# A streaming row normalisation on one core: one queue with a fixed order of whole 8 MB loads and stores

## The chip, the cores and the metric

One core of one Trainium2 chip. The metric is the device time of one execution in microseconds (us). The kernel before took 318.35 us (median of 3 runs, 318.33 to 318.56). The profile that is read here is one execution taken by the hardware profiler; its span (316.9 us for the kernel before) is about 1.5 us shorter than the timed figure.

Names used throughout: L0 to L7 are the eight loads of a tile (8 MB each, HBM to on-chip memory), S0 to S7 the eight stores of the same tiles. A "change of direction" is a place in the queue where a load follows a store or a store follows a load. In the profile lines DVE is VectorE, ACT is ScalarE and SPq the queue of the sync engine; "x4" counts instructions; q1 is the queue that carries the data and q14 the one that fetches instructions, each with packets, MB and share of the time of the 16 DMA engines. The trace does not number the 16 engines: a packet is put to the engine whose packet before ended where this one starts.

## The reference

```
x: float32 [32, 512, 1024]
sums = sum(abs(x), axis=-1, keepdims=True)
out  = x / (sums + 1e-8)
```

Each of 16,384 rows of 1,024 numbers is divided by its sum of absolute values. 67.1 MB are read and 67.1 MB written; there is little arithmetic.

## The kernel before

A tile is 128 partitions x 16 rows x 1,024 numbers: 64 KB in each partition, 8 MB in all. There are three buffers, so at most three tiles are on the chip. The scheduler of the framework decides in which order the queue of the sync engine gets the transfers.

```python
BUFS = 3
# ...
def process_chunk(x_tile, out_ap, r0, rN, mv):
    s = stats.tile([P, rN], mybir.dt.float32, tag="s")
    nc.vector.tensor_reduce(out=s[:, :], in_=x_tile[:, r0 : r0 + rN, :],
        axis=mybir.AxisListType.X, op=mybir.AluOpType.add, apply_absolute_value=True)
    inv = stats.tile([P, rN], mybir.dt.float32, tag="inv")
    nc.vector.reciprocal(out=inv[:, :], in_=s[:, :])
    for r in range(rN):
        # rows r < mv on VectorE (tensor_scalar_mul), the others on ScalarE (activation Copy, scale)
        # ...
    nc.sync.dma_start(out=out_ap[:, r0 : r0 + rN, :], in_=x_tile[:, r0 : r0 + rN, :])

MV = 10
for i in range(ntiles):
    x_tile = sbuf.tile([P, R, d], x.dtype)
    nc.sync.dma_start(out=x_tile[:, :, :], in_=x_t[i, :, :, :])
    if i < ntiles - 2:
        process_chunk(x_tile, out_t[i], 0, R, MV)
    else:                                   # last two tiles: four quarters, each stored by itself
        C = 4
        for c0 in range(0, R, C):
            process_chunk(x_tile, out_t[i], c0, C, (MV * C) // R)
```

The order that came out of it in the queue is L0 L1 L2 S0 S1 S2 L3 L4 L5 S3 S4 S5 L6 L7, then S6 and S7 in quarters: 5 changes of direction.

## Time and profile before

| what | kernel before |
|---|---|
| timed, median | 318.35 us |
| span of the profile | 316.9 us |
| DMA engines busy (16 engines) | 98.6% |
| VectorE busy | 190.8 us, 60% |
| ScalarE busy | 56.7 us, 18% |

The page of the kernel before: the DMA rows over 40 equal slices of the span (tenths busy, then GB/s), the queues, and the chain that ended last.

```profile
DMA  9999999999999999999999999999999999999797
GB/s 397 397 397 513 414 397 397 397 438 488 397 397 505 422 397 397 521 405 397 480 447 397 397 489 438 397 430 480 414 397 480 438 405 422 399 431 432 335 430 331
...
q1 hardware_dynamic: 3168, 134.22, 98.6%
q14 instruction: 2, 0.02, 0.0%
...
DVE 57%; DMA 35%; issue 4%; ACT 0%; ACTq 0%; SPq 0%; DVEq 0%
```

The transfers are the limit: the DMA row is full from the first slice nearly to the last. That the chain names VectorE for 57% does not contradict this; it follows semaphores, and while VectorE worked on one tile the queue was still moving others. A packet is booked in the slice where it starts, so single slices swing around the mean of 424 GB/s.

The same kernel in stretches around its tail. Columns: from:to, length, busy time of VectorE, ScalarE and GpSimd with instructions, granted clock, DMA share, GB/s.

```profile
292.00:294.00 2.00, 2.00 (x4) 0.00 (x0) 0.00 (x0) 1.00 0.86 369
294.00:296.00 2.00, 2.00 (x4) 1.85 (x2) 0.00 (x0) 1.00 0.67 287
296.00:298.00 2.00, 2.00 (x1) 2.00 (x3) 0.00 (x0) 1.00 0.94 393
...
300.00:302.00 2.00, 1.97 (x5) 0.75 (x1) 0.00 (x0) 1.00 0.81 344
```

Near 294 and 300 us the DMA engines run dry for a moment: VectorE is busy throughout and the next quarter store is not ready. This is the only visible idle time after the start.

The groups of instructions by shape: busy us and mean ns of one, then idle time before and its releaser.

```profile
L37 DVE TENSOR_REDUCE s<-x_tile 128x16 f32<-128x16384 f32 x6 | 103.3, 17214 | 67.4 <-DMA x_tile<-in_x_dram 67.4
L54 ACT ACTIVATE x_tile<-x_tile,inv 128x1024 f32<-128x1024 f32 x52 | 55.4, 1137 | 223.9 <-DVE inv L45 223.9
L48 DVE TENSOR_SCALAR x_tile<-x_tile,inv 128x1024 f32<-128x1024 f32 x76 | 51.4, 748 | 0.3
L37 DVE TENSOR_REDUCE s<-x_tile 128x4 f32<-128x4096 f32 x8 | 35.0, 4399 | 43.8 <-DMA x_tile<-in_x_dram 43.8
```

A reduction of a quarter costs 4.40 us, a row 0.75 us on VectorE (0.67 when they follow each other) and 1.14 us on ScalarE. Small changes of the arithmetic can be costed from these.

### The profile page before, as it was taken

Reading aid. Unit: us, or ns where it says so; the run is one execution under the profiler, and the core shown is the slowest. Engines: PE = TensorE matmul, PEld = TensorE weight load, DVE = VectorE, ACT = ScalarE, POOL = GpSimd, SP = SyncE. Lnnn points to the kernel's source line nnn. Section 1 sums busy time; section 2 is a strip of 40 time slices with the busy share of each in tenths; the row PEclk is TensorE's granted clock in tenths of the full one; section 3 lists DMA queues with packets and bytes.
Section 4 is the critical chain, followed back from the end, with each engine's and each line's share of the span. In section 5 each row is a group of like instructions: output and inputs, shape, how many; then the busy total and the mean of one; then the engine's idle time right before and its main releaser. Section 6 shows DMA issues by size and latency. Waiting matters only on the chain.

```text
span 316.9 us, 261 instructions
## 1 busy us (share of the span) xinstructions
DVE 190.8 (60%) x104; ACT 56.7 (18%) x53; POOL 0.2 (0%) x4
## 2 busy tenths in 40 slices
DVE  0019999999990000039999999980000069999910
ACT  0010080080080000000160070080000002522520
POOL 0000000000000000000000000000000000000000
DMA  9999999999999999999999999999999999999797
GB/s 397 397 397 513 414 397 397 397 438 488 397 397 505 422 397 397 521 405 397 480 447 397 397 489 438 397 430 480 414 397 480 438 405 422 399 431 432 335 430 331
DMA packets 3170, 134.24 MB, mean 424 GB/s; under 512 B 352, under 2 KB 352, under 8 KB 352
## 3 DMA queue, kind: packets, MB, share of 16 engines
q1 hardware_dynamic: 3168, 134.22, 98.6%
q14 instruction: 2, 0.02, 0.0%
HBM read 67.11 MB, written 67.11 MB: 424 GB/s over the span
## 4 chain that ended last, share of the span: by engine, by line
DVE 57%; DMA 35%; issue 4%; ACT 0%; ACTq 0%; SPq 0%; DVEq 0%
DVE s L37 41%; DMA x_tile<-in_x_dram 35%; DVE x_tile L48 15%; DVE inv L45 1%; ACT x_tile L54 0%; ACTq L99 0%; SPq L60 0%; DVEq L45 0%; DVEq L48 0%
## 5 line engine op out<-in xcount | busy, mean ns | idle before, releaser
L37 DVE TENSOR_REDUCE s<-x_tile 128x4 f32<-128x4096 f32 (+1 forms) x14 | 138.3, 9891 | 111.2 <-DMA x_tile<-in_x_dram 111.2
L54 ACT ACTIVATE x_tile<-x_tile,inv 128x1024 f32<-128x1024 f32 x52 | 55.4, 1137 | 223.9 <-DVE inv L45 223.9
L48 DVE TENSOR_SCALAR x_tile<-x_tile,inv 128x1024 f32<-128x1024 f32 x76 | 51.4, 748 | 0.3
L54 ACT ACT_TABLE_LOAD x1 | 1.3, 1283 | 22.8 <-DMA x_tile<-in_x_dram 22.8
L45 DVE RECIPROCAL inv<-s 128x4 f32<-128x4 f32 (+1 forms) x14 | 2.6, 200 | 0.4
L88 POOL MEMSET const-bfloat16-1.0<- 128x1 bf16 x1 | 0.1, 101 | 0.0
L88 POOL MEMSET const-uint8-127<- 128x1 uint8 x1 | 0.1, 101 | 0.0
L88 POOL MEMSET const-float32-0.0<- 128x1 f32 x1 | 0.1, 98 | 0.2 <-issue 0.2
L88 POOL MEMSET const-float32-1.0<- 128x1 f32 x1 | 0.1, 98 | 0.0
## 6 DMA issues: line engine op xcount, KB each, us to landing
out_dram<-x_tile SPq DMA_DIRECT2D x8, 2048.0 KB, 9.9
x_tile<-in_x_dram SPq DMA_DIRECT2D x8, 51.0
out_dram<-x_tile SPq DMA_DIRECT2D x6, 29.5
```

What stands on the lines that cost most here:

```text
L37: nc.vector.tensor_reduce(out=s[:, :], in_=x_tile[:, r0 : r0 + rN, :], axis=mybir.AxisListType.X, op=mybir.AluOpType.add, apply_absolute_v ...
L45: nc.vector.reciprocal(out=inv[:, :], in_=s[:, :])
L48: nc.vector.tensor_scalar_mul(out=x_tile[:, r0 + r, :], in0=x_tile[:, r0 + r, :], scalar1=inv[:, r : r + 1],)
L54: nc.scalar.activation(out=x_tile[:, r0 + r, :], in_=x_tile[:, r0 + r, :], func=mybir.ActivationFunctionType.Copy, scale=inv[:, r : r + 1],)
L88: nc = _bacc.Bacc("TRN2", target_bir_lowering=False, num_devices=1)
```

## The change

Its intent: fix the order of the transfers by hand, so that each is a whole 8 MB transfer and so that each store and each load is ready when its turn comes. The last two loads go ahead of the third-last store (the exchange at the end of the plan). All tiles are computed in four chunks, with three rows of four on VectorE, and the epsilon of the reference is added.

```diff
-    stats = ctx.enter_context(tc.tile_pool(name="stats", bufs=BUFS))
+    stats = ctx.enter_context(tc.tile_pool(name="stats", bufs=4))
@@ compute, for every tile
+    C = 4
+    DVE_ROWS = 3
+        for c0 in range(0, R, C):
             # ... tensor_reduce of 4 rows
+            nc.vector.tensor_scalar_add(out=s[:, :], in0=s[:, :], scalar1=EPS)
             # ... reciprocal; 3 rows on VectorE, 1 on ScalarE
@@ order
+    plan = [("L", i) for i in range(BUFS)]
+    for i in range(ntiles):
+        plan.append(("S", i))
+        nxt = i + BUFS - 1
+        if BUFS <= nxt < ntiles:
+            plan.append(("L", nxt))
+    last = max(k for k, p in enumerate(plan) if p[0] == "L")
+    before = plan[last - 1]
+    plan[last - 1], plan[last] = plan[last], before
+    with tc.manual_schedule():
+        for what, i in plan:
+            if what == "L":
+                load(i)
+                compute(i)
+            else:
+                store(i)
```

The resulting order is L0 L1 L2 S0 S1 L3 S2 L4 S3 L5 S4 L6 L7 S5 S6 S7: 9 changes of direction.

More of the change, by code (lines that the diff above doesn't have):

```diff
@@ L7 @@
 from concourse._compat import with_exitstack
+FP32 = mybir.dt.float32
+EPS = 1e-8
 @with_exitstack
@@ L26 @@
     ntiles = n // (P * R)
+    BUFS = 3
     x_t = x_flat.rearrange("(n p r) d -> n p r d", p=P, r=R)
     out_t = out_flat.rearrange("(n p r) d -> n p r d", p=P, r=R)
-    BUFS = 3
     sbuf = ctx.enter_context(tc.tile_pool(name="sbuf", bufs=BUFS))
-    stats = ctx.enter_context(tc.tile_pool(name="stats", bufs=BUFS))
-    def process_chunk(x_tile, out_ap, r0, rN, mv):
-        s = stats.tile([P, rN], mybir.dt.float32, tag="s")
-        nc.vector.tensor_reduce(
-            out=s[:, :],
-            in_=x_tile[:, r0 : r0 + rN, :],
-            axis=mybir.AxisListType.X,
-            op=mybir.AluOpType.add,
-            apply_absolute_value=True,
-        )
-        inv = stats.tile([P, rN], mybir.dt.float32, tag="inv")
-        nc.vector.reciprocal(out=inv[:, :], in_=s[:, :])
-        for r in range(rN):
-            if r < mv:
-                nc.vector.tensor_scalar_mul(
-                    out=x_tile[:, r0 + r, :],
-                    in0=x_tile[:, r0 + r, :],
-                    scalar1=inv[:, r : r + 1],
-                )
-            else:
-                nc.scalar.activation(
-                    out=x_tile[:, r0 + r, :],
-                    in_=x_tile[:, r0 + r, :],
-                    func=mybir.ActivationFunctionType.Copy,
-                    scale=inv[:, r : r + 1],
-                )
-        nc.sync.dma_start(out=out_ap[:, r0 : r0 + rN, :], in_=x_tile[:, r0 : r0 + rN, :])
@@ L62, with load @@
-    MV = 10
-    for i in range(ntiles):
-        x_tile = sbuf.tile([P, R, d], x.dtype)
-        nc.sync.dma_start(out=x_tile[:, :, :], in_=x_t[i, :, :, :])
-        if i < ntiles - 2:
-            process_chunk(x_tile, out_t[i], 0, R, MV)
-        else:
-            C = 4
-            for c0 in range(0, R, C):
-                process_chunk(x_tile, out_t[i], c0, C, (MV * C) // R)
+    stats = ctx.enter_context(tc.tile_pool(name="stats", bufs=4))
+    tiles = {}
+    def load(i):
+        x_tile = sbuf.tile([P, R, d], FP32)
+        nc.sync.dma_start(out=x_tile[:, :, :], in_=x_t[i])
+        tiles[i] = x_tile
@@ new lines, in store, with compute @@
+    def store(i):
+        nc.sync.dma_start(out=out_t[i], in_=tiles[i][:, :, :])
+    C = 4
+    DVE_ROWS = 3
+    def compute(i):
+        x_tile = tiles[i]
+        for c0 in range(0, R, C):
+            s = stats.tile([P, C], FP32)
+            nc.vector.tensor_reduce(
+                out=s[:, :],
+                in_=x_tile[:, c0 : c0 + C, :],
+                axis=mybir.AxisListType.X,
+                op=mybir.AluOpType.add,
+                apply_absolute_value=True,
+            )
+            nc.vector.tensor_scalar_add(out=s[:, :], in0=s[:, :], scalar1=EPS)
+            inv = stats.tile([P, C], FP32)
+            nc.vector.reciprocal(out=inv[:, :], in_=s[:, :])
+            for r in range(C):
+                row = x_tile[:, c0 + r, :]
+                if r < DVE_ROWS:
+                    nc.vector.tensor_scalar_mul(out=row, in0=row, scalar1=inv[:, r : r + 1])
+                else:
+                    nc.scalar.activation(
+                        out=row,
+                        in_=row,
+                        func=mybir.ActivationFunctionType.Copy,
+                        scale=inv[:, r : r + 1],
+                    )
```

## The prediction

> **What bounds it now.** The DMA engines. The page's DMA row reads 9 in nearly all of 40 slices, and the queue table gives 98.6% of 16 engines' span (316.9 us) for 134.22 MB. Reading the packet records of the trace one by one: a 64 KB packet takes 2.418 us, a 16 KB packet 0.611 us. That is 27.1 GB/s per engine, 434 GB/s for 16, beside the 435 GB/s that the Trainium skill, "DMA: Bandwidth & Descriptors", section Specifications, calls the fabric ceiling: the trace agrees.
>
> So the floor is 128 packets of 64 KB per engine: 128 x 2.418 = 309.5 us. The other 7.4 us of the span, from the packet records:
> - start, until the first packets flow: about 2.0
> - first 16 packets slow (about 3.1 us each): 0.7
> - first change from loads to stores, at 58 us: 16 packets of about 3.65 us: 1.2
> - slow packets at later changes of direction: 0.5
> - idle at 293 and at 300 us, where quarter stores were not yet ready: 1.2 in the mean
> - 16 KB packets instead of 64 KB (4 x 0.611 against 2.418): 0.4
> - end, from last packet to end of span: 1.3
>
> The chain of waits says 57% VectorE, but the queue always held more work. VectorE is busy 190.8 us (60%).
>
> **What the change does.**
> 1. The queue becomes L0 L1 L2 S0 S1 L3 S2 L4 S3 L5 S4 L6 L7 S5 S6 S7, whole 8 MB transfers of 19.35 us. Saves 0.4, and, if nothing stalls, the 1.2 idle.
> 2. Direction changes go from 5 to 9. Later ones cost about 0.1 each: adds 0.4.
> 3. VectorE: reduces in four pieces, 4 x 4.39; 12 rows instead of 10 (0.672 each in sequence); four reciprocals at 0.17 and four epsilon adds, estimated at 0.17 too, plus gaps of 0.03. About 27.1 us per tile against 24.2; total about 217 us. ACT drops to 32 x 1.137 = 36 us. All hidden while a tile's load plus store take 38.7.
>
> **Is there a stall?** By queue position, with starts above: L2 ends near 61, S0 is ready at 50, S1 at 77, before its turn at 81. L3 waits for S0's landing at 81, with S1 behind it in the queue until 100. Later transfers are ready in time until the last. L6, twelfth, lands at about 237; tiles 6 and 7 need 54.2 us of VectorE, so S7 is issued at about 291.3 and flows 1 to 1.8 us later (as the first load did). S6 ends at about 294.3. Margin: 1 to 2 us. Without the swap, L7 would land 19.35 us later and S7 come about 7 us late.
>
> **Predicted:** 2.0 + 309.5 + 2.7 + 1.3, about 315.6 us of span, plus 1.45 (318.35 timed against 316.9 profiled): 317.0 us, 0.4% less. 8 in 10: 315.9 to 318.9. Faster by over 2% 0.01 (312 lies below floor plus start and end), within 2% 0.97, slower 0.02.
>
> **What would show it.** DMA share near 99%; packets of 64 KB only at 2.418 us; no gaps after the first packet, the last store following S6 without one; VectorE near 217 us; about 24 us after the last VectorE row rather than 13.
>
> **What would make it wrong.** A tile's compute above about 27.8 us: each us more shows twice in the tail, less the margin. Direction changes costing 1.2 us like the one at 58: up to 9 us more.

## The result

The changed kernel took 319.82 us (median of 5, 319.55 to 320.08) beside 318.40 us for the kernel before (318.33 to 318.67). The ratio is 1.0042 (95% interval 1.0030 to 1.0055). Ratios here and below are the mean time of one kernel's fast runs over that of the other's of the same rounds, so not quite the ratio of the medians. Run again later on another occasion, the changed kernel gave 1.0028 (1.0016 to 1.0040). So the change makes it 0.3 to 0.4% slower, where 0.4% faster (317.0 us) was predicted.

The page of the changed kernel, the same lines:

```profile
DMA  9999999999999999999999999999999999999996
GB/s 387 404 396 511 412 396 420 371 478 437 404 413 486 420 396 437 470 404 404 429 470 404 429 462 429 396 437 470 412 420 453 445 388 445 478 396 396 412 404 264
...
q1 hardware_dynamic: 2304, 134.22, 98.4%
q14 instruction: 2, 0.02, 0.0%
...
DVE 51%; DMA 29%; another core or an unknown queue 11%; issue 1%; DVEq 0%; SPq 0%
```

The DMA row looks as full as before, and 864 packets fewer (3,168 to 2,304: no quarter stores) bring no gain.

The tail of the changed kernel, before its last store and at its end:

```profile
292.00:294.00 2.00, 1.83 (x4) 0.59 (x1) 0.00 (x0) 1.00 0.76 328
294.00:296.00 2.00, 1.48 (x3) 0.56 (x1) 0.00 (x0) 1.00 0.23 98
296.00:298.00 2.00, 0.00 (x0) 0.00 (x0) 0.00 (x0) 1.00 1.23 524
...
313.00:314.00 1.00, 0.00 (x0) 0.00 (x0) 0.00 (x0) 1.00 2.27 983
314.00:315.00 1.00, 0.00 (x0) 0.00 (x0) 0.00 (x0) 1.00 0.15 66
```

Two things are to be seen. First, there is an idle gap before S7 after all (DMA share 0.23 from 294 to 296 us). Second, look at the last two lines: 983 GB/s for 1 us is fifteen 64 KB packets that start in the same microsecond, and 66 GB/s for 1 us is exactly one more packet, about 1 us later. One of the 16 DMA engines runs behind the others, and it ends the kernel.

Its groups of instructions:

```profile
L54 DVE TENSOR_REDUCE s<-x_tile 128x4 f32<-128x4096 f32 x32 | 141.2, 4413 | 73.6 <-DMA x_tile<-in_x_dram 73.6
L67 DVE TENSOR_SCALAR x_tile<-x_tile,inv 128x1024 f32<-128x1024 f32 x96 | 66.5, 749 | 1.1
L69 ACT ACTIVATE x_tile<-x_tile,inv 128x1024 f32<-128x1024 f32 x32 | 36.8, 1150 | 233.5 <-DVE inv L63 233.5
L63 DVE RECIPROCAL inv<-s 128x4 f32<-128x4 f32 x32 | 5.7, 178 | 3.0
L61 DVE TENSOR_SCALAR s<-s 128x4 f32<-128x4 f32 x32 | 5.4, 170 | 1.1
```

The arithmetic is as costed: VectorE 216.6 us in all against 217 predicted, an epsilon addition 0.17 us. And two lines of its timeline (start us, us, engine):

```profile
229.13 66.75 SPq L45 DMA_DIRECT2D out_dram<-x_tile  x3
...
239.98 4.42 DVE L54 TENSOR_REDUCE s<-x_tile 128x4 f32<-128x4096 f32 x1 [10.91 <-DMA x_tile<-in_x_dram]
```

VectorE could begin tile 6 at 239.98 us, where 237 had been expected, and S7, the last of the three stores in the first line, was issued at 295.5 (229.13 + 66.75 less its own 0.33) instead of 291.3.

The trace records when each of the 16 DMA engines has landed its share of a transfer. The distance between the first and the last of the 16 is the spread of the engines:

| spread of the 16 landings, us, by position in the queue | 1st | 4th | 8th | 12th | 14th | last |
|---|---|---|---|---|---|---|
| kernel before | 0.75 | 0.75 | 0.75 | 0.67 | 1.61 | 0.18 (a quarter) |
| changed kernel | 0.86 | 1.08 | 2.66 | 3.75 | 3.42 | 1.12 |

In the kernel before the spread stays under 1.1 us until the last loads, and falls from 1.67 to 0.25 us at 300 us, where all engines wait for a quarter store and start afresh. In the changed kernel it grows to 3.75 us. A load counts as landed only when the slowest engine is done. The Trainium skill, "DMA: Bandwidth & Descriptors", section "Why a DMA increments its semaphore by 16 and not by 1", says this: only the full count of 16 means that all data landed. The trace agrees: the twelfth transfer (L6) landed on its first engine at 236.21 us and on its last at 239.95, and VectorE began at 239.98.

### The profile page after: what moved, and what is told of

Same layout as the page of the kernel before. It is cut to its first block, busy times and chain, and to the rows that moved or that the text cites. A ratio compares the mean times of both kernels' runs of the same rounds, so it can differ in the third digit from the quotient of the medians.

```text
span 318.0 us, 336 instructions
## 1 busy us (share of the span) xinstructions
DVE 216.6 (68%) x192; ACT 38.1 (12%) x33; POOL 0.2 (0%) x4
## 3 DMA queue, kind: packets, MB, share of 16 engines
q1 hardware_dynamic: 2304, 134.22, 98.4%
## 4 chain that ended last, share of the span: by engine, by line
DVE 51%; DMA 29%; another core or an unknown queue 11%; issue 1%; DVEq 0%; SPq 0%
DVE s L54 33%; DMA x_tile<-in_x_dram 19%; DVE x_tile L67 15%; DMA out_dram<-x_tile 10%; DVE inv L63 1%; DVE s L61 1%; DVEq L118 0%; DVEq L63 0%; SPq L45 0%
## 5 line engine op out<-in xcount | busy, mean ns | idle before, releaser
L54 DVE TENSOR_REDUCE s<-x_tile 128x4 f32<-128x4096 f32 x32 | 141.2, 4413 | 73.6 <-DMA x_tile<-in_x_dram 73.6
L67 DVE TENSOR_SCALAR x_tile<-x_tile,inv 128x1024 f32<-128x1024 f32 x96 | 66.5, 749 | 1.1
L69 ACT ACTIVATE x_tile<-x_tile,inv 128x1024 f32<-128x1024 f32 x32 | 36.8, 1150 | 233.5 <-DVE inv L63 233.5
L63 DVE RECIPROCAL inv<-s 128x4 f32<-128x4 f32 x32 | 5.7, 178 | 3.0
L61 DVE TENSOR_SCALAR s<-s 128x4 f32<-128x4 f32 x32 | 5.4, 170 | 1.1
```

Of the source, the lines that this page charges most:

```text
L54: nc.vector.tensor_reduce(out=s[:, :], in_=x_tile[:, c0 : c0 + C, :], axis=mybir.AxisListType.X, op=mybir.AluOpType.add, apply_absolute_va ...
L61: nc.vector.tensor_scalar_add(out=s[:, :], in0=s[:, :], scalar1=EPS)
L67: nc.vector.tensor_scalar_mul(out=row, in0=row, scalar1=inv[:, r : r + 1])
L69: nc.scalar.activation(out=row, in_=row, func=mybir.ActivationFunctionType.Copy, scale=inv[:, r : r + 1],)
```

## The experiments

Theory A: the engines drift apart, at changes of direction above all, and the latest one sets the end. Rival B: the idle gap before S7 is the loss. Theory C came up on the way: instruction fetches delay one engine. The kernels of one group ran on one chip beside the kernel before, with 5 rounds except where 3 is said. "Late by" is how much later the last of the 16 engines landed its share of the last transfer than the middle one.

### Transfers alone, with 9, 5, 13 and 1 changes of direction

All arithmetic is taken out, three fixed buffers are loaded and stored in a written order, and the output is a copy or worse, wrong.

```diff
-    # compute(i) after each load
+    plan = [("L", 0, 0), ("L", 1, 1), ("L", 2, 2), ("S", 0, 0), ...]   # what, tile, buffer
+    with tc.manual_schedule():
+        for what, i, b in plan:
+            if what == "L":
+                nc.sync.dma_start(out=T[b][:, :, :], in_=x_t[i])
+            else:
+                nc.sync.dma_start(out=out_t[i], in_=T[b][:, :, :])
# nc9:  L0 L1 L2 S0 S1 L3 S2 L4 S3 L5 S4 L6 L7 S5 S6 S7   (the changed kernel's order)
# nc5:  L0 L1 L2 S0 S1 S2 L3 L4 L5 S3 S4 S5 L6 L7 S6 S7   (the old order, whole stores)
# nc13: L0 L1 S0 L2 S1 L3 S2 L4 S3 L5 S4 L6 S5 L7 S6 S7
# nc1:  L0 ... L7 S0 ... S7, buffers reused
```

nc9:

> Transfers alone (no arithmetic, output wrong on purpose: it is a copy), in the changed kernel's order, 9 changes of direction. Theory A (changes of direction make one or two DMA engines late, and the latest engine sets the end): about 319.5 us, little below the changed kernel's 319.8, latest engine 2 to 4 us behind the median. Rival B (the 1.3 to 2.3 us idle before the last store, from arithmetic that ended late, is the loss): about 317.8 us, since nothing waits for arithmetic.

nc5:

> Transfers alone, whole 8 MB transfers in the old kernel's order, 5 changes of direction. A: about 1.5 us below nc9 (near 317.8), latest engine about 1 us behind the median. B: the same as nc9 within 0.4 us.

nc13:

> Transfers alone, loads and stores in turn, 13 changes of direction. A: 1.5 us or more above nc9 (near 321). B: the same as nc9 within 0.4 us.

nc1:

> Transfers alone, all loads and then all stores, 1 change of direction, some tiles stored twice and others not at all (output wrong on purpose). A: 1 to 2 us below nc5 (near 316.5). B: the same as nc9 within 0.4 us. If the 16 slow packets of about 3.65 us at 58 us belong to the first change from loads to stores, they move to about 157 us; if they belong to the time since the start, they stay at 58.

| run | changes | median us | range | ratio to before (95%) | middle engine's last landing | late by |
|---|---|---|---|---|---|---|
| nc1 | 1 | 315.88 | 315.76 to 316.09 | 0.9917 (0.9904 to 0.9929) | 313.08 | 0.29 |
| nc5 | 5 | 317.86 | 317.03 to 318.12 | 0.9971 (0.9958 to 0.9983) | 313.82 | 1.47 |
| nc9 | 9 | 319.34 | 318.25 to 319.62 | 1.0019 (1.0005 to 1.0033) | 314.47 | 2.06 |
| nc13 | 13 | 320.21 | 318.87 to 320.40 | 1.0046 (1.0032 to 1.0060) | 314.25 | 3.57 |

The ends of nc1, nc5 and nc13, the same three stretches of each:

```profile
309.00:312.00 3.00, 0.00 (x0) 1.00 0.81 350
312.00:313.00 1.00, 0.00 (x0) 1.00 0.01 0
...
315.00:316.00 1.00, 0.00 (x0) 1.00 0.00 0
```

```profile
309.00:312.00 3.00, 0.00 (x0) 1.00 0.91 393
312.00:313.00 1.00, 0.00 (x0) 1.00 0.15 66
...
315.00:316.00 1.00, 0.00 (x0) 1.00 0.00 0
```

```profile
309.00:312.00 3.00, 0.00 (x0) 1.00 0.91 393
312.00:313.00 1.00, 0.00 (x0) 1.00 0.91 393
...
315.00:316.00 1.00, 0.00 (x0) 1.00 0.15 66
```

With 1 change no packet starts after 312 us; with 5 one does; with 13 a single packet starts in 315 to 316 us, at least 2 us after the last of the others. Middle engines land within 1.4 us of each other across all four kernels, while the times differ by 4.3 us. Nothing waits for arithmetic here, so B cannot make this difference; A holds. The step from 9 to 13 changes was smaller than expected (0.9 us, not 1.5 or more), and nc9 did not repeat well later (see below). Side result: the sixteen packets of about 3.65 us at 58 us belong to the first change from loads to stores. They were the last load packet of each engine, and moved to 38.5 us in nc13 and to 155 us in nc1 (where they took about 3.1 us).

### The gap before S7 taken away, fewer changes, no exchange, and a pause at each change

noeps: the epsilon addition removed, which shortens the chain of VectorE before S7.

```diff
-            nc.vector.tensor_scalar_add(out=s[:, :], in0=s[:, :], scalar1=EPS)
```

> The changed kernel without the epsilon additions. The chain of VectorE work before the last store gets 8 x 0.27 = 2.2 us shorter, about the idle time (1.3 to 2.3 us) before the last store, which should nearly vanish. Theory A (the latest engine sets the end, and it had no idle time): at most 0.5 us faster, 319.3 to 319.8. Rival B (the idle time counts): 317.8 to 318.3.

319.94 us (318.68 to 320.24), ratio 1.0044, a little above the expected range. The gap was nearly gone:

```profile
294.00:296.00 2.00, 0.00 (x0) 0.00 (x0) 0.00 (x0) 1.00 0.53 229
296.00:298.00 2.00, 0.00 (x0) 0.00 (x0) 0.00 (x0) 1.00 1.08 463
```

(Packets are booked where they start; counted from the packet records, the idle time before S7 is 0.15 us in the mean instead of 1.5.) The time did not move, and the last engine landed 2.98 us after the middle one. B falls: the gap made thirteen engines wait, while the three latest, one of which ends the kernel, were still busy with S6. Both instruction fetches of this run (98 and 296 us, see below) fell on the engine that ended last. No cost of the epsilon is seen.

grouped22: 5 changes with the exchange kept, two rows of four on ScalarE.

```diff
-    DVE_ROWS = 3
+    DVE_ROWS = 2
-    plan = ...
+    plan = "L0 L1 L2 S0 S1 S2 L3 L4 L5 S3 S4 L6 L7 S5 S6 S7"
```

> The changed kernel with 5 changes of direction instead of 9 (order L0 L1 L2 S0 S1 S2 L3 L4 L5 S3 S4 L6 L7 S5 S6 S7, still with the last two loads ahead of the third-last store) and with two rows of four on ScalarE, which takes 5.4 us from the VectorE chain of the last two tiles, so that the last store is ready before its turn. Theory A: as the transfers alone with 5 changes, 317.2 to 318.2, faster than both kernels, no idle time before the last store. If changes of direction did not matter once arithmetic runs: 319.3 or more.

319.17 us (318.61 to 319.75), ratio 1.0023 (1.0011 to 1.0035): below the changed kernel's 1.0042 and 1.0028, but not clear of the second, and 1 us above the expected range. A miss, and the lead to C. The page counts 3 packets on the instruction queue:

```profile
q14 instruction: 3, 0.02, 0.0%
```

The engine that ends last is the one that served two of them: each time a 0.30 us hole between two data packets, with a fetch of 8,192 bytes (0.309 us) in it, and the next data packet 0.35 us too long.

noswap (3 rounds): the exchange at the end of the plan left out.

```diff
-    plan[last - 1], plan[last] = plan[last], before
+    del before
```

> The changed kernel without the exchange (last load behind the third-last store). From the measured pieces: the last load lands at about 277.5 us, its tile takes 27.8, so the last store starts near 306 instead of 296 us, and about 9 to 10 us of idle time stand before it on all 16 engines: about 328.5 us. The prediction on record had said 7 us late.

329.69 us (329.16 to 330.24), ratio 1.0355. As expected within about 1.2 us. Its tail:

```profile
295.00:300.00 5.00, 4.83 (x7) 1.15 (x1) 0.00 (x0) 1.00 0.03 13
300.00:305.00 5.00, 4.83 (x4) 0.22 (x1) 0.00 (x0) 1.00 0.00 0
```

The DMA engines stand still while VectorE works on the last tile. So the exchange is worth about 10 us within this order.

nc9sync (3 rounds): nc9's order, with the buffers chosen so that the first transfer after each change of direction reads or writes the tile of the transfer just before it, and so waits for its landing.

```diff
# buffer of each transfer
-L0.0 L1.1 L2.2 S0.0 S1.1 L3.0 S2.2 L4.1 S3.0 L5.2 S4.1 L6.0 L7.1 S5.2 S6.0 S7.1
+L0.0 L1.1 L2.2 S0.2 S1.0 L3.0 S2.0 L4.0 S3.0 L5.0 S4.0 L6.0 L7.1 S5.1 S6.0 S7.2
```

> Transfers alone in the changed kernel's order, but at each of the 9 changes of direction the first transfer waits until the last of the other direction has landed (it reads or writes the same tile), so that no engine still runs one direction while another runs the other (output wrong on purpose). If late engines come from two directions running at once: no packets over 2.5 us except right after each pause, the engines' spread does not grow from change to change, and the pauses cost 2 to 3 us each: 335 to 345 us. If a change slows packets by itself: the spread still grows to over 1.5 us.

332.79 us (332.62 to 332.9), ratio 1.0452. The time is below the expected 335 to 345 us, since the pauses were cheaper: 14.7 us of idle time per engine, 1.6 per pause. The spread never passed 0.9 us and was 0.17 at the end. The 3.65 us packets of the first change vanished, and stores after a pause had almost no slow packets (0.1 us at most in the mean); loads after a pause had one per engine, 0.6 to 0.7 us too long, like the first load of all. This supports that engines are slowed where loads and stores are in flight together. It is not proof for every change, since a pause also lets the engines start level again.

### Instruction fetches

nc5instr: nc5 with 600 idle instructions; nc5b: nc5 again beside it.

```diff
+        for k in range(600):  # nothing waits for these
+            nc.vector.memset(idle[:, k : k + 1], 0.0)
```

> nc5 (transfers alone, 5 changes of direction) with 600 tiny memsets on VectorE that nothing waits for. Theory C: 8 KB instruction fetches (queue q14 of the page), one about every 128 instructions of an engine, all fall on one DMA engine and cost it about 0.65 us each (0.31 for the fetch, 0.35 for the packet behind it), and this engine ends last. About 5 fetches in the span, the latest engine 2 us or more further behind the median than in nc5b, the time 1 to 3 us above nc5b. If fetches are harmless: within 0.4 us of nc5b.

> nc5 once more, for comparison on the same chip: 317 to 318.1 us, no instruction fetch in the span.

nc5instr 321.52 us (321.23 to 321.86), ratio 1.0091; nc5b 317.31 us (316.85 to 318.51), ratio 0.9962. Two lines of nc5instr, the instruction queue on its page and its very end:

```profile
q14 instruction: 5, 0.04, 0.0%
```

```profile
313.00:314.00 1.00, 0.00 (x0) 0.00 (x0) 1.00 0.01 0
314.00:315.00 1.00, 0.00 (x0) 0.00 (x0) 1.00 0.15 66
...
316.00:317.00 1.00, 0.00 (x0) 0.00 (x0) 1.00 0.15 66
```

After 313 us only one engine still works, with one packet at a time. The five fetches came at 7, 13, 19, 25 and 31 us; the spread was 4.15 us after the first load, 5.5 after the third, and 5.9 at the end: nothing gives the time back in between. All five fell on one engine, and they cost (1.0091 - 0.9962) x 318.67 = 4.1 us, 0.8 us each, more than the 1 to 3 us expected. C holds. The Trainium skill, "DMA: Bandwidth & Descriptors", section "Queues, rings and completion order", has half of what is needed to see this coming: queue row 14 belongs to the runtime, and each engine takes turns between its rows a whole packet at a time. The trace agrees: the fetch stands between two data packets of one engine. The other half is in "Runtime: NRT & Kernel Launch", section "Instruction fetch mechanics": an engine's sequencer refills its instruction memory through a DMA queue of its own while it runs. The trace agrees in that, too: the five fetches are on q14 and the data on q1, and the first four come while the memsets run.

When do fetches come? The trace does not say which compute engine a fetch serves; it is inferred from how many instructions each had begun by then. In nc5instr, where VectorE alone has many, the first four come 128 instructions apart. In the other kernels they fit VectorE having begun 50 to 65 instructions, and again 180 to 196, and ScalarE 55 to 70. So the number of instructions decides it, though not to the instruction. By this count the old kernel has one fetch of VectorE (187 us) and one of ScalarE (283 us), and they fell on two different DMA engines; the changed kernel has two of VectorE (88 and 262 us), and both fell on one.

before_shorttail: the old kernel with the VectorE multiplications of its last two tiles left out. Its output is wrong, which doesn't matter for the time.

```diff
+            if r < mv and skip:   # skip=True for the last two tiles
+                continue
```

> The old kernel with the VectorE multiplications of its last two tiles left out (half of their rows stay unscaled, output wrong on purpose), so that its quarter stores are ready before their turn and the idle time at 293 and 300 us goes. The prediction on record counted that idle time as 1.2 us of loss: 317.2. Theory A (the latest engine, 1.6 us behind at that point, sets the end, and the idle time only lets it catch up): 317.7 to 318.5.

318.25 us (317.57 to 318.85), ratio 0.9988 (0.9975 to 1.0001). Its idle time was gone (0.04 us per engine in the mean), its spread stayed at 1.25 us to the end instead of falling to 0.18, and the gain was 0.4 us, not clear of zero. So the 1.2 us of idle time in the old kernel were worth about 0.4 us, and by the interval 0.8 us at most.

grouped_few: few changes and few instructions together; it gives the right result.

```diff
-        for c0 in range(0, R, C):            # four chunks per tile
-            # reduce, add, reciprocal, 2 rows VectorE, 2 rows ScalarE
+        # one tensor_reduce, one add, one reciprocal for the 16 rows
+        if i < 3:  # 8 rows one by one on VectorE
+        else:      # 8 rows in one tensor_tensor with inv broadcast
+        # 8 rows on ScalarE
```

> grouped22 with one reduction, epsilon addition and reciprocal per tile, 8 rows on VectorE (from the fourth tile on in one instruction) and 8 on ScalarE, so that VectorE has about 53 instructions and ScalarE 64. Theory C: one instruction fetch in the span instead of three, 317.8 to 318.4, below grouped22's 319.2 and not slower than the old kernel. If fetches are harmless: about 319.2.

316.97 us (316.66 to 318.12), ratio 0.9948 (0.9935 to 0.9960). Faster than both kernels, and 0.8 us below the expected range.

### Order and fetches in the full kernel

after_few: grouped_few with the changed kernel's order put back. grouped_few2 is grouped_few again.

```diff
-    plan = "L0 L1 L2 S0 S1 S2 L3 L4 L5 S3 S4 L6 L7 S5 S6 S7"
+    plan = ...   # the changed kernel's, 9 changes
```

> grouped_few with the changed kernel's order put back (9 changes of direction), else the same. If the order costs with arithmetic what it costs with transfers alone: 1 to 2 us above grouped_few2, about 318.5. If the whole difference to the changed kernel came from instruction fetches: within 0.4 us of grouped_few2, about 317.

> grouped_few once more for comparison on the same chip: 316.6 to 317.6 us, faster than the kernel before by 0.3 to 0.7%.

after_few 318.35 us (317.02 to 319.36), ratio 0.9993 (0.9974 to 1.0013); grouped_few2 317.06 us (316.88 to 317.48), ratio 0.9954 (0.9942 to 0.9967). The order costs about 1.2 us with arithmetic too. grouped_few2's queues on its page:

```profile
q1 hardware_dynamic: 2304, 134.22, 99.0%
q14 instruction: 1, 0.01, 0.0%
```

after_few_instr: after_few with 26 idle memsets in each of the first six tiles; after_few2, nc9b and after2 are after_few, nc9 and the changed kernel again, on the same chip.

```diff
+        for k in range(26 if i < 6 else 0):
+            nc.vector.memset(idle[:, 26 * i + k : 26 * i + k + 1], 0.0)
```

> after_few with 26 tiny memsets on VectorE in each of the first six tiles (156 in all, nothing waits for them, about 1.6 us of VectorE per tile where it has time to spare). Two more instruction fetches than after_few (3 in place of 1). If fetches cost time in the full kernel: 0.6 to 2 us above after_few2, near 319.5 to 320. If not: within 0.4 us of after_few2.

> after_few once more: 317.8 to 319. If its gain over nc9 was chance, it comes out at or above nc9b.

> nc9 once more: 318.5 to 319.6. If arithmetic in itself costs nothing, within 0.5 us of after_few2.

> The changed kernel itself beside the others on one chip: 319.5 to 320, 0.5 us or more above nc9b.

| run | median us | range | ratio to before (95%) |
|---|---|---|---|
| after_few_instr | 319.10 | 318.83 to 319.65 | 1.0022 (1.0010 to 1.0034) |
| after_few2 | 317.44 | 316.77 to 318.37 | 0.9970 (0.9958 to 0.9982) |
| nc9b | 317.27 | 316.52 to 319.49 | 0.9970 (0.9946 to 0.9994) |
| after2 | 319.44 | 318.99 to 319.73 | 1.0028 (1.0016 to 1.0040) |

The queue line of after_few_instr:

```profile
q14 instruction: 3, 0.02, 0.0%
```

after_few2, nc9b and after2 came out below what had been expected of them, nc9b by over 1 us. Three readings. The added fetches (3 instead of 1 in the span) cost (1.0022 - 0.9970) x 318.5 = 1.7 us, 0.8 us each, as in nc5instr. In the profiled run the two added ones (69 and 223 us) fell on one DMA engine, and it ended last; the third, which after_few has too and which by the count is ScalarE's (262 us), fell on one that did not. No cost of arithmetic as such is seen: after_few2 and nc9b are equal, though the interval of nc9b is 0.8 us to each side. And nc9's first result was partly chance: the same kernel gave 1.0019 and 0.9970, and its single runs lie 3 us apart. How far an engine falls behind differs from run to run, so the price of the order is only an average: from 5 to 9 changes 0.0028 of the time with transfers alone (means of the two results each), or 0.9 us, and 0.0031 with arithmetic (after_few against grouped_few, two results each), or 1.0 us. The single pairs with transfers alone are far apart: 0.0048 for nc9 against nc5, which ran on one chip, and 0.0008 for nc9b against nc5b, which did not.

## Why the prediction was wrong

What was right:

- The bound: DMA engines, 2.418 us per 64 KB packet, 309.5 us for 128 of them on each engine. The 435 GB/s of the Trainium skill ("DMA: Bandwidth & Descriptors", section Specifications) fits 434 measured in both kernels.
- The start, the first slow packets (0.69 us against 0.7) and the first change (1.24 against 1.2).
- The arithmetic: VectorE 216.6 us against 217; all hidden but for the last tile.
- That the exchange is needed, though its worth was put at 7 us and is about 10.

What was wrong:

1. "Later changes cost about 0.1 each: adds 0.4." This is the term that failed, and with it the way of adding: the sum "2.0 + 309.5 + 2.7 + 1.3" took means over the 16 engines. The mean of all extra packet time came out at 3.35 us against 2.7: the eight later changes took about 1.3 us in the mean, 0.16 each, where the record has 0.9 in all (0.5 + 0.4). But the span ends with the latest engine, and there they took 3.05 us, 0.4 each, nearly all in the first packet of L4 and the last packets of L3, L4 and L5; its first packet (0.8) and the first change (1.4) were nearly as predicted. In the profiled run of the changed kernel that engine never waited; its own sum is a start at 2.47, 309.5 of packets, 4.9 of slow packets (5.3 counted as above, less 0.4 by which the records of successive packets overlap) and 1.16 to the end: 318.0 us, the measured span. That is 2.2 us more of slow packets than the 2.7, 0.5 from the start, and 0.1 less at the end. The remaining 0.3 of the 2.8 us error is the step from span to timed figure (1.8 us, not 1.45). The record had named dear changes of direction as what could make it wrong, at 1.2 us each; on the latest engine they cost a third of that.
2. "If nothing stalls, the 1.2 idle" saved, with 0.4 for the packets. Idle time of the other engines is no loss while one engine is late. Taken out of the old kernel alone, it gave about 0.4 us, not clear of zero (before_shorttail); the quarter stores let all engines start level at 300 us, and the change took that away.
3. "Margin: 1 to 2 us" before S7. The margin failed: L6 landed at 239.95 instead of 237, because its slowest engine was 3.7 us behind its first, and two tiles took 55.5 us instead of 54.2. The gap that followed was of 1.3 to 2.3 us on thirteen engines. No gain came from taking it away (noeps).

So the expected gain went to the latest engine. Two causes of lateness are shown: four more changes of direction cost about 1 us on average, and each instruction fetch about 0.8 us in the runs that added some (in their profiles the engine with the fetches ended last). The changed kernel has two fetches like the old one, but both on one DMA engine, and nothing that levels the engines after them. In its first profiled run, the fetches fell on an engine that did not end last; in the run repeated later they fell on the one that did.

From the changed kernel (1.0042 and 1.0028) to after_few (0.9993 and 0.9970) there are about 1.7 us. after_few lacks both fetches of VectorE, and its one fetch (261 us) did not fall on the engine that ended last. When two fetches of VectorE were added to it, the 1.7 us came back: after_few_instr (1.0022) is within 0.2 us of the changed kernel beside it (after2, 1.0028).

What stays open: in the first profiled run of the changed kernel the engine that ended last had no fetch, so the fetches did not set the end of that run, and the price of a fetch can only be an average, too. Why loads and stores in flight together slow single packets is not settled either.

## What to carry to other kernels

When a kernel is bound by DMA, ask for the latest of the 16 engines and not for the mean: look at how far apart the engines land one transfer, and whether that distance grows. Here few changes of direction and few instructions on the compute engines kept it small: with both (grouped_few) the kernel took 317 us, where the changed kernel took 319.8. The old kernel, at 318.4, has the same five changes, but two fetches and the quarter stores; what each of these is worth in it was not taken apart. Idle time that all engines but the last one have is not a cost, so removing it is not a gain.

## What the Trainium skill lacked or had wrong

- "DMA: Bandwidth & Descriptors", section Specifications, gives about 358 GB/s as the HBM limit of a core, and its section Bandwidth says that this side binds for transfers between HBM and on-chip memory, beside a measurement of 425 for one core alone; it gives the 358 as what each of two streaming cores gets. One core moved 424 GB/s over the whole span here, and 434 while packets ran undisturbed, so the 358 did not bind, and the row in Specifications needs the condition. What the other core of the pair would take was not tried.
- "Runtime: NRT & Kernel Launch", section "Instruction fetch mechanics", gives refills of 16 KiB for 256 instructions and calls their cost mostly hidden. In these traces a fetch is 8,192 bytes, about one per 128 instructions of an engine, and in a kernel bound by DMA it is not hidden: 0.8 us each (nc5instr, after_few_instr), because the fetches of one compute engine fell on one of the 16 DMA engines that move the data (VectorE's in nc5instr; in grouped22 ScalarE's fetch fell on another DMA engine than VectorE's two).
- No page that was read for this has the cost of changing between loads and stores in one queue. Here the first change cost 1.2 us in the mean over the engines (0.7 in nc1), and four more later ones about 1 us in the time, through one late engine.
- None of them was found to say that the 16 engines drift apart in a long stream and do not come level by themselves: landings 3.75 us apart in the changed kernel, 0.18 us after a common wait in the old one.
- "DMA: Bandwidth & Descriptors" gives about 0.6 us to the first byte on this path, and does not say from where it counts. Here S7 started about 0.9 us after its issuing instruction began and 0.5 to 0.6 after that instruction ended, which would fit. The first load did not: its instruction ran from 0.73 to 1.11 us, and its first packets started between 1.74 and 2.66 us, by engine.
